# Attention's value products one loop step later, with operands shifted against their weights and gmlp pieces in another order

## The chip, the cores and the metric

The kernel runs on one core of one Trainium2 chip. The metric is the device time of one execution in microseconds. Engines: PE is TensorE (PEld its weight loads), DVE is VectorE, ACT is ScalarE, POOL is GpSimd, SP is SyncE, which here issues nearly all DMAs.

## What is computed

One layer of a decoder for 1,024 prompt positions and 64 sample positions (8 sequences of 8) that share weights, everything in float32. Of the reference, what bears on the change:

```python
h = rmsnorm(x, norm_mix)
q, k, v, gu, gv, ga, gb = split_in(h @ w_in)      # 16 query heads, 4 key/value heads of 64
o = attn_prompt(q, k, v, sinks)                   # window 128, blocks of 128 queries, 256 keys
s = spatial_gating(gelu(gu), layernorm(gelu(gv)), ws, bs)
merged = sigmoid(ga) * (o @ w_pa) + sigmoid(gb) * (s @ w_pb)
x = x + merged @ w_out
x = x + conv_ffn(rmsnorm(x, norm_ffn), ...)
```

In prompt attention a block of 128 queries sees its own block of keys up to the diagonal and the previous block's keys above it, so each query sees exactly 128 keys.

## The kernel before

A float32 product is made of three products in a rounded 32-bit form: every operand is split into a high part (a copy, on ScalarE) and a low part (a subtraction, on VectorE), and `wh*h + wh*l + wl*h` are summed in PSUM. Large products with 7 sub-products per tile pair come before and after; the change touches the stage between them, about 460 to 690 us into the span.

The positions are two groups: group 0 has the 64 sample positions and prompt blocks 0 to 3 (576 columns), group 1 prompt blocks 4 to 7 (512 columns). `attention(gr, pieces)` runs once for each group. It first does the sample attention (group 0 only), then a loop over 16 steps (4 key/value heads by 4 blocks), software-pipelined. In loop step i:

- `tr_p` transposes step i-2's normalized probabilities (four 128x128 transposes into the one bank `pt`), and splits them into `ph` (ScalarE) and `pl` (VectorE). From both GpSimd selects `c` with four affine selects: scores of one half of the previous and one half of the own block lie in the same 128 columns, and `c` holds, for the half where the two mix, the entries that belong to the other block.
- `sc_p` scores step i: eight matmuls with queries as weights and keys `kst` streaming into the one score buffer `sc`; a copy to `s` (ScalarE), a masked copy of the previous block's scores over it (VectorE), a maximum (VectorE), four exponentials (ScalarE), a reciprocal and a scaling (VectorE).
- `pv_p` multiplies step i-2's `ph` and `pl` by the values `vst` (four matmuls) and `c` by the difference of neighbouring blocks' values `dvst` (two matmuls), into the one bank `po`; then a copy (ScalarE), two additions and the split of the output (`oh`, `ol`).

In front of and behind `sc_p` stands `fill()`, which works off a list of pieces of other work, so that TensorE has something to do: as many as `slots["at"] * n // slots["of"]` says. For group 0 the pieces are the gmlp branch's products: `branch(c)` gives eight pieces for output tile c, four for each position group, each with nine matmuls; the first fetches the weight tile (`W.get`, which also casts the next one and loads further ones), the last of each group multiplies by the gate tile and stores the product to DRAM (`mbd`). The gate tile is loaded by `sg_load` into one of the four buffers of `stg`. For group 1 the pieces are the merge products of group 0's attention output.

Keys, queries and values of the next head are loaded from DRAM by `operands(kv + 1)` and `values(kv + 1)` within the steps of the current head; each has two buffers. The values were written to DRAM (`vd`, and their differences `dvd`) some 400 us earlier, one store for each block, in `v_out`.

The order of instructions on each engine's queue isn't the program's text alone: a scheduler reorders the text's instructions by what it takes to be ready, keeping the dependencies. `gap(pool, n)` is an unused tile of n bytes per partition, which moves the tiles behind it.

Of the kernel before, what the change touches and what calls it, by code (L numbers as in the profile page):

```python
# [6 lines left out]
F32 = mybir.dt.float32  # L7
# [8 lines left out]
P = 128  # L16
D = 1024
KD = 8
# [16 lines left out]
def layer(tc, a):  # L35
# [11 lines left out]
    with ExitStack() as top:  # L47
# [287 lines left out]
        vd = dr("vd", [P, NKV, 8, P])  # L335
        v3d = dr("v3d", [P, 256])
        dvd = dr("dvd", [P, NKV, 8, P])
# [14 lines left out]
        with ExitStack() as ph1:  # L352
# [175 lines left out]
            def v_out(g, i, ps):  # L528
# [7 lines left out]
                else:  # L536
# [3 lines left out]
                    for to, x in ((vd, v), (dvd, None)):  # L540
# [11 lines left out]
                        nc.sync.dma_start(to[:, :, name], t)  # L552
# [367 lines left out]
            def prepare(gr):  # L920
# [8 lines left out]
                def operands(kv):  # L929
                    def go():  # L930
                        if kv < NKV:
                            t = gr["kst"][kv] = kvp.tile([P, 2, nk], F32R, name="kst", bufs=2)
                            r = 64 * (kv % 2)
# [9 lines left out]
                def values(kv):  # L943

                    def go():
                        if kv < NKV:
# [3 lines left out]
                            nc.sync.dma_start(v.bitcast(F32), vd[:, kv, b0:b0 + nv])  # L950
                            for e in (0, 64):
                                for o in (0, 64):
                                    nc.sync.dma_start(d[o:o + 64, e // 64].bitcast(F32),
                                                      dvd[e:e + 64, kv, b0 + 1:b0 + 1 + nd])
# [77 lines left out]
            def sg_load(c):  # L1032
                for g in range(2) if c < KD else ():
                    n, off = groups[g]["n"], groups[g]["off"]
                    t = sgs[c, g] = stage(n)
                    nc.sync.dma_start(t, sgd[1][c][:, off:off + n])

            def branch(c):
# [3 lines left out]
                def part(g, e, k0):  # L1042
                    n, off, base = (groups[g][x] for x in ("n", "off", "base"))

                    def go():
# [4 lines left out]
                        if g == e == 0 and k0:  # L1050
                            sg_load(c + 1)
# [30 lines left out]
            def attention(gr, pieces):  # L1082
# [6 lines left out]
                slots = {"n": len(pieces), "done": 0, "at": 0, "of": 40 + (8 if has_s else 0)}  # L1089
# [99 lines left out]
                with tc.tile_pool(name=f"at{g}", bufs=1) as ap:  # L1189
                    steps = [(kv, i) for kv in range(NKV) for i in range(nblk)]  # L1190
                    st = {}

                    def sc_p(kv, i):
# [15 lines left out]
                        if i == 2:  # L1209
                            gr["values"](kv + 1)()  # L1210
                        s = ap.tile([P, 4, P + 1], F32, name="s", bufs=3)
# [18 lines left out]
                    def tr_p(kv, i):  # L1230
# [4 lines left out]
                        ph = ap.tile([P, 512], F32R, name="ph")  # L1235
                        pl = ap.tile([P, 512], F32R, name="pl")
                        split(ph, pl, pt)
                        parts = []
                        if gr["blk0"] + i:
                            c = ap.tile([P, 512], F32R, name="c")  # L1240
# [36 lines left out]
                    for i in range(len(steps) + 2):  # L1277
                        if i >= 2:
# [4 lines left out]
                        fill()  # L1283
                        if i >= 2:
                            pv_p(*steps[i - 2])
# [9 lines left out]
            sg_load(0)  # L1295
# [643 lines left out]
```

## Time and profile before

| | |
|---|---|
| time, median of 3 runs | 1530.84 us (1525.71 to 1532.65) |
| time of the profiled execution | 1529.31 us |
| its span | 1527.6 us |
| granted TensorE clock | 0.996 |
| PE busy | 1507.0 us (99%) |
| PEld busy | 1489.1 us (97%) |
| DVE busy | 1156.2 us (76%) |
| ACT busy | 823.2 us (54%) |
| POOL busy | 274.9 us (18%) |

The span is the time from the first to the last instruction of one profiled execution. A busy PE isn't PE at its peak, as matmuls are pipelined: idle weight loads and the mean duration of a matmul tell more. In a group's row, L and a number is the line of the kernel before, then engine, operation, output and inputs by the program's names, shapes, count, busy time, mean of one in ns, and the idle time of the engine just before them with what ended it. "A <- B: x, n, y" says that A waited for B for x us in all, n times, y at most. A row of one tile's instructions gives minimum, median and maximum of their durations.

### The profile page before, as it was taken

The numbers are of one execution on the slowest core, as the hardware profiler recorded it, in microseconds if no ns is written. First come the engines' busy times: TensorE is split into PE (matmuls) and PEld (weight loads), VectorE is DVE, ScalarE is ACT, GpSimd is POOL, SyncE is SP. The second block draws the span as 40 slices with busy tenths as digits, with TensorE's granted clock in tenths as the row PEclk, the third lists the DMA queues.
The fourth block names the chain that finished last, engine by engine and source line by source line (L and its number), as shares of the span: only waits on it lengthen the run. The fifth ranks groups of instructions, "written<-read, shape, count | busy, mean of one in ns | idle before, by whom it ended". The sixth has DMA issues, their size and how long they took to land.

```text
span 1527.6 us, 31403 instructions
## 1 busy us (share of the span) xinstructions
PE 1507.0 (99%) x12202; PEld 1489.1 (97%) x12202; DVE 1156.2 (76%) x1918; ACT 823.2 (54%) x1745; POOL 274.9 (18%) x429
## 2 busy tenths in 40 slices
PE   9999999999999999999999999999999999999998
PEld 9999999999998999989999999999999999999997
DVE  6886778756544886889658888898899888785685
ACT  6555764454543674774433555555555556453562
POOL 0000002200120232440122212232232222000002
PEclk9999999999999999999999999999999999999998
DMA  8553447747649857658988432332243226973453
GB/s 285 156 170 126 166 168 257 247 140 270 222 152 327 258 187 217 202 181 301 327 275 275 146 120 92 120 137 100 87 151 107 79 93 214 363 258 96 127 177 130
DMA packets 136357, 286.64 MB, mean 188 GB/s; under 512 B 15248, under 2 KB 43344, under 8 KB 136208
## 3 DMA queue, kind: packets, MB, share of 16 engines
q1 hardware_dynamic: 132176, 281.08, 55.2%
q10 hardware_dynamic: 4032, 3.55, 0.7%
q8 instruction: 96, 1.57, 0.4%
q14 instruction: 53, 0.43, 0.1%
HBM read 195.69 MB, written 90.85 MB: 188 GB/s over the span
## 4 chain that ended last, share of the span: by engine, by line
PE 68%; DVE 5%; ACT 4%; issue 3%; POOL 2%; DMA 2%; SPq 0%; POOLq 0%; ACTq 0%; DVEq 0%
PE st L294 40%; PE dn L1700 13%; PE mm L235 12%; ACT s L1224 2%; POOL c L1245 1%; POOL x L1765 1%; PE sc L1205 1%; PE mx L832 1%; DVE pl L41 1%; DVE nm L1221 1%; DVE s L1227 0%; ACT ot L1268 0%; DVE wl L41 0%; DVE of L1273 0%; DMA wraw<-wpb 0%
## 5 line engine op out<-in xcount | busy, mean ns | idle before, releaser
L294 PE MATMUL st<-th,wh 128*128 128x256 f32 (+1 forms) x2128 | 611.3, 287 | 4.2 <-ACT k L275 2.3
L294 PE MATMUL st<-tl,wh 128*128 128x256 f32 (+1 forms) x2128 | 609.4, 286 | 0.0
L294 PE MATMUL st<-th,wl 128*128 128x256 f32 (+1 forms) x2128 | 608.8, 286 | 0.0
L294 PEld LDWEIGHTS st<-th,wh 128*128 128x128 f32 x2128 | 400.7, 188 | 6.0 <-ACT k L275 3.4
L294 PEld LDWEIGHTS st<-th,wl 128*128 128x128 f32 x2128 | 401.0, 188 | 0.0
L294 PEld LDWEIGHTS st<-tl,wh 128*128 128x128 f32 x2128 | 400.5, 188 | 0.0
L40 ACT CAST wh<-wraw 128x512 fp32r<-128x512 f32 (+2 forms) x204 | 139.6, 694 | 107.0 <-PE st L294 35.4
L41 DVE TENSOR_TENSOR wl<-wraw,wh 128x512 fp32r<-128x512 f32 (+2 forms) x204 | 159.4, 794 | 37.7 <-ACT wh L40 35.5
L1700 PE MATMUL dn<-th,wh 128*128 128x288 f32 (+1 forms) x616 | 176.7, 287 | 0.0
L1700 PE MATMUL dn<-tl,wh 128*128 128x288 f32 (+1 forms) x616 | 176.2, 286 | 0.0
L1700 PE MATMUL dn<-th,wl 128*128 128x288 f32 (+1 forms) x616 | 175.1, 284 | 0.0
L40 ACT CAST wh<-ws 128x512 fp32r<-128x512 f32 x160 | 98.1, 622 | 96.8 <-PE st L294 62.0
L41 DVE TENSOR_TENSOR wl<-ws,wh 128x512 fp32r<-128x512 f32 x160 | 109.5, 697 | 48.5 <-ACT wh L40 46.8
L1700 PEld LDWEIGHTS dn<-th,wl 128*128 128x128 f32 x616 | 115.9, 188 | 0.0
L1700 PEld LDWEIGHTS dn<-tl,wh 128*128 128x128 f32 x616 | 115.7, 188 | 0.0
L1700 PEld LDWEIGHTS dn<-th,wh 128*128 128x128 f32 x616 | 115.6, 188 | 0.0
L282 POOL TENSOR_TENSOR z<-kn,k 128x256 f32<-128x256 f32 (+1 forms) x32 | 29.9, 938 | 320.0 <-ACT kn L277 304.4
L40 ACT CAST th<-traw 128x544 fp32r<-128x544 f32 (+1 forms) x85 | 53.8, 642 | 45.1 <-PE dn L1700 32.6
L41 DVE TENSOR_TENSOR tl<-traw,th 128x544 fp32r<-128x544 f32 (+1 forms) x85 | 61.6, 732 | 21.0 <-ACT th L40 20.6
L235 PE MATMUL mm<-s,wh 128*128 128x256 f32 (+1 forms) x384 | 75.4, 292 | 0.9 <-DMA s<-sd 0.9
L525 PE MATMUL st<-w2h,th 128*128 128x256 f32 x308 | 74.4, 283 | 0.4 <-ACT w2h L40 0.4
L235 PE MATMUL mm<-oh,wh 128*128 128x256 f32 (+1 forms) x256 | 74.0, 289 | 0.0
(292 smaller groups left out, 3178.2 us busy)
## 6 DMA issues: line engine op xcount, KB each, us to landing
wraw<-wt SPq DMA_DIRECT2D x133, 512.0 KB
traw<-td SPq DMA_DIRECT2D x77, 272.0 KB
td<-za SPq DMA_DIRECT2D x22, 544.0 KB
wraw<-wt SPq DMA_DIRECT2D x35, 256.0 KB
upd<-hl SPq DMA_DIRECT2D x14, 512.0 KB
td<-t SPq DMA_DIRECT2D x11, 544.0 KB
qd<-q SPq DMA_DIRECT2D x8, 576.0 KB
q<-qd SPq DMA_DIRECT2D x8, 576.0 KB
```

What stands on the lines that cost most here:

```text
L40: S.copy(hi, src)
L41: V.tensor_sub(lo, src, hi.bitcast(F32))
L235: PE.matmul(ps[:, lo:lo + c1 - c0], u[:, k, :], v[:, c0:c1], start=(k == 0 and i == 0), stop=(k == nk - 1 and i == 2))
L282: op(to, pick(x, to, lo, hi), pick(y, to, lo, hi))
L294: PE.matmul(ps, u[:, kk, :], v, start=first and kk + i == 0, stop=kk == 3 and i == 2, skip_group_check=True)
L525: PE.matmul(ps, u, v[:, k, :], start=k + i == 0, stop=k == KD - 1 and i == 2)
L832: PE.matmul(ps[:, P * i:P * i + P], vn[:, i], late["wst"][:, c, :], start=True, stop=True)
L1205: PE.matmul(ps[:, h, o0:256], q, kst[kv][:, e, k0:cur + P], start=e == 0, stop=e == 1)
L1221: V.tensor_reduce(nm, s, AX.X, ALU.max, negate=True)
L1224: S.activation(s[:, h], s[:, h], AF.Exp, bias=nm[:, h:h + 1], accum_out=dn[:, h:h + 1])
L1245: G.affine_select(cs[w:w + 64, :, e], src[r:r + 64, :, e].bitcast(F32), [[0, 4], [1 - 2 * e, 64]], ALU.is_ge, 0.0, base=-e, channel_multip ...
L1700: PE.matmul(place(m, e), u[:, m, :], v[:, lo:hi], start=new and i + k == 0 and (e == 0 or m % 2 == 0), stop=i == NU - 1 and k == 2, skip_g ...
```

## The change

1. In attention's loop `pv_p` works on step i-3 instead of i-2; the loop has one step more, `ph`, `pl` and `c` have two buffers, the next head's values are requested at its fourth block instead of the third, and the number of slots grows from 40 to 41.
2. `vd` and `dvd` are laid out by block: [8, P, NKV, P] instead of [P, NKV, 8, P].
3. A gap of 64 bytes behind the first key tile, gaps of 256 and 128 bytes ahead of attention's own tiles, and rows of `s` of 132 instead of 129 elements.
4. The gmlp pieces run for two output tiles c, c+1 at a time: group 0 of both, then group 1 of both. The gate tile of a tile and group is loaded at its own first piece, no longer in pairs within the tile before.

```diff
-        vd = dr("vd", [P, NKV, 8, P])
+        vd = dr("vd", [8, P, NKV, P])
...
-        dvd = dr("dvd", [P, NKV, 8, P])
+        dvd = dr("dvd", [8, P, NKV, P])
...
-                        nc.sync.dma_start(to[:, :, name], t)
+                        nc.sync.dma_start(to[name], t)
...
                             t = gr["kst"][kv] = kvp.tile([P, 2, nk], F32R, name="kst", bufs=2)
+                            if kv == 0:
+                                gap(kvp, 64)
...
-                            nc.sync.dma_start(v.bitcast(F32), vd[:, kv, b0:b0 + nv])
+                            nc.sync.dma_start(v.bitcast(F32), vd[b0:b0 + nv, :, kv].rearrange("b p d -> p b d"))
                             for e in (0, 64):
                                 for o in (0, 64):
                                     nc.sync.dma_start(d[o:o + 64, e // 64].bitcast(F32),
-                                                      dvd[e:e + 64, kv, b0 + 1:b0 + 1 + nd])
+                                                      dvd[b0 + 1:b0 + 1 + nd, e:e + 64, kv].rearrange(
+                                                          "b p d -> p b d"))
...
-            def sg_load(c):
-                for g in range(2) if c < KD else ():
-                    n, off = groups[g]["n"], groups[g]["off"]
-                    t = sgs[c, g] = stage(n)
-                    nc.sync.dma_start(t, sgd[1][c][:, off:off + n])
+            def sg_load(c, g):
+                n, off = groups[g]["n"], groups[g]["off"]
+                t = sgs[c, g] = stage(n)
+                nc.sync.dma_start(t, sgd[1][c][:, off:off + n])
...
-                        if g == e == 0 and k0:
-                            sg_load(c + 1)
+                        if e == k0 == 0:
+                            sg_load(c, g)
...
-                slots = {"n": len(pieces), "done": 0, "at": 0, "of": 40 + (8 if has_s else 0)}
+                slots = {"n": len(pieces), "done": 0, "at": 0, "of": 41 + (8 if has_s else 0)}
...
+                    gap(ap, (256, 128)[g])
...
-                        if i == 2:
+                        if i == 3:
                             gr["values"](kv + 1)()
-                        s = ap.tile([P, 4, P + 1], F32, name="s", bufs=3)
+                        s = ap.tile([P, 4, 132], F32, name="s", bufs=3)[:, :, 0:P + 1]
...
-                        ph = ap.tile([P, 512], F32R, name="ph")
-                        pl = ap.tile([P, 512], F32R, name="pl")
+                        ph = ap.tile([P, 512], F32R, name="ph", bufs=2)
+                        pl = ap.tile([P, 512], F32R, name="pl", bufs=2)
...
-                            c = ap.tile([P, 512], F32R, name="c")
+                            c = ap.tile([P, 512], F32R, name="c", bufs=2)
...
-                    for i in range(len(steps) + 2):
-                        if i >= 2:
+                    for i in range(len(steps) + 3):
+                        if 2 <= i < len(steps) + 2:
                             tr_p(*steps[i - 2])
                         fill()
                         if i < len(steps):
                             sc_p(*steps[i])
-                        fill()
-                        if i >= 2:
-                            pv_p(*steps[i - 2])
+                        if i < len(steps) + 2:
+                            fill()
+                        if i >= 3:
+                            pv_p(*steps[i - 3])
...
-            sg_load(0)
-            attention(groups[0], [x for c in range(KD) for x in branch(c)])
+            parts = [branch(c) for c in range(KD)]
+            attention(groups[0], [x for c in range(0, KD, 2) for g in (0, 4) for d in (0, 1) for x in parts[c + d][g:g + 4]])
```

## The prediction

> **What bounds the kernel now.** I read the page's busy line first, then a table of stretches around attention, then who the weight loads waited for, then the groups of matmuls by shape, then the chain of work.
>
> ```profile
> span 1527.6 us, 31403 instructions
> PE 1507.0 (99%) x12202; PEld 1489.1 (97%) x12202; DVE 1156.2 (76%) x1918; ACT 823.2 (54%) x1745; POOL 274.9 (18%) x429
> ```
>
> TensorE has work in flight nearly all the time, so no part of the change can win more than TensorE's own stalls and slow matmuls in the stage that it touches. That stage is attention, one stretch for each position group:
>
> ```profile
> core 0: us, PE busy (x) PEld busy (x) DVE busy (x) ACT busy (x) POOL busy (x), PEclk, DMA share, GB/s
> 500.00:582.00 82.00, 80.17 (x615) 75.67 (x615) 70.21 (x131) 59.72 (x192) 25.67 (x61) 1.00 0.63 209
> 600.00:687.00 87.00, 84.43 (x622) 78.80 (x621) 74.98 (x140) 64.08 (x198) 34.86 (x77) 1.00 0.66 204
> ...
> 630.00:660.00 30.00, 29.10 (x215) 27.28 (x213) 27.30 (x53) 23.65 (x75) 13.08 (x30) 1.00 0.76 249
> 688.00:784.00 96.00, 95.95 (x769) 95.90 (x769) 64.92 (x87) 39.84 (x56) 12.44 (x9) 1.00 0.88 311
> ```
>
> Columns after the stretch: its length, then busy time of each engine. The weight loads (PEld) are the better gauge: in the pure product stage 688 to 784 they are busy 95.90 of 96, in attention 75.67 of 82 and 78.80 of 87. So attention leaks about 6 and 8 us in weight loads that stand still. The clock is 1.00 throughout. VectorE is second: 86% of either stretch, and 27.30 of 30 (91%) at its fullest. Whom the loads waited for, from 460 to 690:
>
> ```profile
> PEld po L1265 <- POOL c L1245: 7.6, 25, 1.1
> PEld po L1262 <- DVE pl L41: 1.5, 4, 0.5
> PEld mm L235 <- DMA s<-sd: 1.4, 2, 0.8
> PEld po L1262 <- issue: 1.1, 4, 0.4
> PEld po L1262 <- ACT ph L40: 0.8, 2, 0.5
> ```
>
> The largest by far is the value product waiting for `c`, the part of the probabilities that GpSimd selects for the previous block's difference.
>
> **Term A: value products one step later.** In one loop step the kernel transposes the probabilities of block i-2 (`tr_p`), fills, scores block i (`sc_p`), fills, then multiplies i-2's probabilities with the values (`pv_p`). Between `tr_p` and `pv_p` lies this chain:
>
> ```profile
> L1245 POOL TENSOR_SCALAR_AFFINE_SELECT c<-ph x56: 408/413/877, 508.9 to 684.1; 64x256 fp32r<-64x256 f32 x56
> L1245 POOL TENSOR_SCALAR_AFFINE_SELECT c<-pl x56: 409/412/1279, 510.4 to 685.2; 64x256 fp32r<-64x256 f32 x56
> L40 ACT CAST ph<-pt x32: 567/587/592, 505.4 to 683.0; 128x512 fp32r<-128x512 f32 x32
> L41 DVE TENSOR_TENSOR pl<-pt,ph x32: 675/692/694, 506.3 to 683.8; 128x512 fp32r<-128x512 f32 x32
> ```
>
> With medians: 0.587 (ACT) + 0.692 (VectorE) + 2 x 0.412 (the two selects that need `pl`) = 2.1 us even if every engine is free. VectorE is 86% busy, so it often isn't. After the change a whole step more lies between: there are 32 steps in 82 + 87 us, so about 5.3 us. The chain then has some 8 us and is no longer late. What its lateness costs, from the groups by shape (mean ns, then the idle time before them):
>
> ```profile
> L1265 PE MATMUL po<-c,dvst 128*128 128x256 f32 x56 | 18.4, 353 | 2.7 <-POOL c L1245 1.7
> L1262 PE MATMUL po<-ph,vst 128*128 128x256 f32 x56 | 16.2, 295 | 0.6 <-ACT ph L40 0.2
> L1262 PE MATMUL po<-pl,vst 128*128 128x256 f32 x56 | 15.2, 294 | 0.7 <-DVE pl L41 0.7
> L235 PE MATMUL mm<-mh,wh 128*128 128x256 f32 x192 | 53.5, 279 | 0.0
> L1205 PE MATMUL sc<-kst,q 128*128 128x256 f32 x224 | 32.8, 286 | 0.2 <-ACT s L1213 0.2
> ...
> L1262 PEld LDWEIGHTS po<-ph,vst 128*128 128x128 f32 x56 | 10.6, 189 | 2.1 <-issue 1.1 <-ACT ph L40 0.8 <-ACT s L1213 0.2
> L1262 PEld LDWEIGHTS po<-pl,vst 128*128 128x128 f32 x56 | 10.5, 188 | 1.8 <-DVE pl L41 1.5
> L1265 PEld LDWEIGHTS po<-c,dvst 128*128 128x128 f32 x56 | 10.0, 187 | 8.4 <-POOL c L1245 7.6
> ```
>
> Idle in front of these weight loads: 8.4 + 2.1 + 1.8 = 12.3 us. A load that waited also can't run ahead of the matmul before it, so the matmul behind it shows longer: 56 x (353 - 279) + 56 x (295 - 279) + 56 x (294 - 279) ns = 4.1 + 0.9 + 0.8 = 5.8 us. Upper end 18.1 us.
>
> The lower end comes from VectorE, which does the same work in less time. If it can't go beyond the 91% of its fullest stretch, the two stretches shrink to 70.21 / 0.91 = 77.2 and 74.98 / 0.91 = 82.4, a gain of 4.8 + 4.6 = 9.4 us. Part of VectorE's idleness is itself due to the late products:
>
> ```profile
> ACT ot L1268 <- PE po L1265: 26.2, 19, 2.8
> ```
>
> ```profile
> DVE of L1273 <- ACT ot L1268: 8.3, 12, 1.9
> DVE dn L1226 <- ACT s L1224: 7.6, 11, 1.7
> ```
>
> ScalarE stood 26.2 us in front of the output copy of a product that wasn't there, with the next step's exponentials queued behind it, and VectorE waited for both. So VectorE should get a little past 91%, though not far: I take **11 us**, nearer to the VectorE end, which is 92.5 to 93% of either stretch. What is late next is VectorE's `pl`, which frees the single transpose bank, and its masked copy, which frees the single score bank. One more loop step (19 instead of 18) adds a fill and no work; `ph`, `pl`, `c` double, so the early split waits for no product.
>
> **Term B: 192 modulo 256.** `kst` buffers are 2 x 512 x 4 or 2 x 640 x 4 bytes, queries 2 x 576 x 4 or 2 x 512 x 4, block steps 512 bytes, all multiples of 256. So keys (streamed) and queries (weights) now start a multiple of 256 bytes apart. The gap of 64 bytes behind the first keys changes that; gaps and the wider `s` move the probabilities against the values. If this is why a score matmul shows 286 ns and an equal-sized output product 279, it is worth 224 x 7 ns = 1.6 us at the upper end; the same 7 ns on the 168 value products, 1.2 us more. The lower end is nothing, or as much lost, -2.8 us. I take 0.5, since most of it would hide behind VectorE. The Trainium skill, "TensorE: Matmul & The Clock Gate", Part 2, on loading the stationary operand, gives TensorE two independent read ports, one for the streamed operand and one for the weights, so that neither takes bandwidth from the other; by that rule this part changes nothing, and the sum would be 0.5 us smaller. No row here separates addresses from shapes, so the trace leaves this open.
>
> **Term C: gmlp pieces by group for two tiles.** The chain shows the second group's operands arriving late, and a loader that blocks the queue:
>
> ```profile
> 467.64 5.28 DMA s<-sd
> ...
> 540.20 2.00 DMA mbd<-stg
> 542.22 0.32 SPq L1036
> 542.63 4.44 DMA wraw<-wt
> ```
>
> The new order runs two tiles of group 0 before it touches group 1's operands: four more pieces of 9 matmuls, some 5 us of cover, so the 1.4 us of weight loads waiting for `s` should mostly go. Second, the gate loads now need the buffer of four groups ago instead of the one just stored:
>
> ```profile
> SPq L1036 <- DMA mbd<-stg: 4.2, 6, 1.5
> SPq L950 <- PE po L1265: 7.8, 3, 5.0
> ```
>
> So 4.2 us of queue blocking goes, with weights queued behind it in the lines at 542. Casts for the second weight tile come four pieces after the first instead of eight, and both tiles stay until the pair is done: three of the ring's four slots. Ends: -1 and 2 us; I take 1.
>
> **Term D: values by block.** Stores before attention become one run of 2,048 bytes per partition instead of four of 512; loads become four or five runs of 512 instead of one.
>
> ```profile
> L552 SPq DMA_DIRECT2D vd<-ws x8: 513/516/617, 45.9 to 87.5; - x8
> L950 SPq DMA_DIRECT2D vst<-vd x8: 319/345/631, 475.5 to 646.5; - x8
> L953 SPq DMA_DIRECT2D dvst<-dvd x32: 444/541/1445, 477.3 to 649.1; - x32
> ```
>
> A four-run issue took 516 ns, a one-run issue 345. The value loads should go to about 516: 8 x 0.17 = 1.4 us of SyncE's queue. The 32 difference loads, by the same step, cost 5.4 us of that queue at most; the 15 stores give 2.6 us back. Behind them in the queue stand weights and keys, but these loads are issued four steps (20 us) before their use, as before: the request moves one step later together with the products, and its wait for the products that free the buffer (7.8 us above) keeps its form. On the path I put -0.5 us, between -3 and 1.
>
> **Sum.** 11 + 0.5 + 1 - 0.5 = 12 us. The profiled execution took 1529.31 us beside its span of 1527.6; less 12 is 1517.3. The median of the runs shown (1530.84) lies 1.5 above that execution, so I predict 1518.8 us. The runs before spread over 1525.71 to 1532.65, so half a per cent, 7.65 us, is about what a measurement of this kernel can tell from no change.
>
> **Rivals.**
>
> 1. The wait moves to VectorE. The score and transpose banks are single, so TensorE stops there as soon as VectorE lags. For it: 91% in the fullest stretch. Against it: the waits for VectorE at scores and transposes are below 1 us each now. If only 4 us of A survive and B hides, 4 + 1 - 0.5 = 4.5, so 1526.3: no change that can be told.
> 2. VectorE keeps up entirely, the whole upper end is won: 18.1 + 1.5 + 1 = 20.6, so 1510.2.
> 3. Slower: gate tiles late. They were loaded in pairs a whole tile ahead, now at the first piece of their own group, and the product with them stands in VectorE's strict order ahead of softmax work. Groups follow each other by
>
> ```profile
> 499.53 0.75 DVE L1055 TENSOR_TENSOR stg<-stg,mm 128x576 f32<-128x576 f32 x1 [0.44 <-PE mm L235]
> 587.01 0.69 DVE L1055 TENSOR_TENSOR stg<-stg,mm 128x512 f32<-128x512 f32 x1 [1.01 <-PE mm L235]
> ```
>
>    (587.01 - 499.53) / 11 = 8.0 us, so the load has about 6 us. A small store landed in 2.00 us, a 512 KB weight load in 4.44. It decides from a landing of over 6 us: with 8 us, each of 16 groups holds VectorE 2 us, 32 us in all, against the 12 won: 1530.8 + 20 = 1551. Were half of them late, 1535.
> 4. The change doesn't do what it says: the order of TensorE's queue is planned with assumed costs, and the products are pulled forward again to where `c` is late; then B, C and D remain, 1 us: 1529.8.
>
> **How the numbers follow.** Forecast (1513 to 1523) 0.52; rival 2 0.12; rival 1 0.20; rival 4 0.09; rival 3 0.07. Faster by over half a per cent: forecast and rival 2, 0.64. Same: rivals 1 and 4, 0.29. Slower: 0.07. The range runs from rival 2's 1510 to 1528, which leaves out rival 3, most of rival 4 and the tail of rival 2, under 2 in 10.
>
> **What would show it.** A: the wait of value products for GpSimd's `c` is gone and the c product's mean falls from 353 to about 285 ns; both attention stretches shrink 5 to 6 us, and VectorE's share there rises to about 93%. B: the score matmul's mean falls from 286 toward 279. C: no weight load waits for `s`, no gate load for a store. D: value-load issues near 516 ns and no product waiting for a value DMA. It would be wrong if new waits of scores or transposes on VectorE add up to more than 5 us, or if VectorE waits for a gate tile's DMA.

## The result, and the profile after

| | before | after |
|---|---|---|
| median, first comparison | 1529.7 us (21 runs) | 1524.99 us (21 runs, 1519.64 to 1529.17) |
| ratio, 95% interval | | 0.9966 (0.9955 to 0.9976) |
| median, in a later comparison | 1529.93 us (20 runs) | 1521.57 us (9 runs) |
| ratio, 95% interval | | 0.995 (0.9931 to 0.9969) |
| profiled execution, its span | 1529.31, 1527.6 us | 1525.18, 1523.3 us |

The change makes the kernel faster, by 4.7 us in the first comparison and 8.4 in the later one. The intervals of the two overlap from 0.9955 to 0.9969, some 5 to 7 us. The forecast was 12. Three profiles of the changed kernel end at 1523.3, 1519.3 and 1528.4 us, so single executions say little about 2 or 3 us; the times below are medians against the kernel before on the same chip, and the traces are read for what waits for what.

The page's busy line after, then the stretches of attention (same columns as before):

```profile
span 1523.3 us, 31416 instructions
PE 1500.1 (98%) x12202; PEld 1486.9 (98%) x12202; DVE 1155.1 (76%) x1918; ACT 822.8 (54%) x1745; POOL 273.1 (18%) x429
```

```profile
500.00:582.00 82.00, 78.42 (x627) 75.60 (x626) 70.37 (x132) 60.91 (x193) 29.06 (x64) 1.00 0.66 221
600.00:687.00 87.00, 84.03 (x656) 80.90 (x655) 76.45 (x144) 65.11 (x200) 31.36 (x77) 1.00 0.69 214
```

In the same two stretches TensorE now does 627 + 656 matmuls instead of 615 + 622, 3.7% more. VectorE's share is 86% and 88%; it was 86% and 86%. The forecast had counted on 92.5 to 93%.

Whom TensorE waited for, from 460 to 690 (line numbers of the changed kernel: 1237 is the transposes, 1265 and 1268 the value products):

```profile
PE pt L1237 <- DVE s L1230: 3.1, 5, 1.3
PEld pt L1237 <- ACT ot L1271: 3.0, 3, 1.4
PEld pt L1237 <- issue: 2.4, 6, 1.0
PEld mm L235 <- DMA s<-sd: 2.2, 1, 2.2
...
PEld po L1265 <- issue: 1.6, 3, 0.7
PEld pt L1237 <- DVE pl L41: 1.1, 2, 0.7
PE po L1265 <- DVE of L1276: 1.0, 3, 0.5
...
PE pt L1237 <- DVE pl L41: 0.7, 2, 0.5
...
PEld sc L1208 <- DVE s L1218: 0.2, 1, 0.2
```

The wait for GpSimd's `c` that led the list before (7.6 us) is gone, and the transposes have taken its place. The groups by shape, from 490 to 690 (mean ns, then idle before):

```profile
L1268 PE MATMUL po<-c,dvst 128*128 128x256 f32 x56 | 11.2, 281 | 0.0
L1265 PE MATMUL po<-ph,vst 128*128 128x256 f32 x56 | 15.4, 296 | 2.1 <-DVE of L1276 1.0 <-ACT s L1216 0.6 <-ACT s L1227 0.4
L1265 PE MATMUL po<-pl,vst 128*128 128x256 f32 x56 | 14.6, 282 | 0.0
L1208 PE MATMUL sc<-kst,q 128*128 128x256 f32 x224 | 32.0, 283 | 0.0
L1237 PEld LDWEIGHTS pt<-c_ident,s 128*128 128x128 f32 x128 | 13.9, 141 | 7.4 <-ACT ot L1271 3.0 <-issue 2.4 <-DVE pl L41 1.1
L1265 PEld LDWEIGHTS po<-ph,vst 128*128 128x128 f32 x56 | 10.5, 188 | 3.3 <-issue 1.6 <-ACT s L1216 0.8 <-ACT s L1227 0.6
L1265 PEld LDWEIGHTS po<-pl,vst 128*128 128x128 f32 x56 | 10.6, 189 | 0.0
L1268 PEld LDWEIGHTS po<-c,dvst 128*128 128x128 f32 x56 | 8.6, 189 | 0.0
```

The loads of the value products stood 12.3 us before and 3.3 now, and the c product takes 281 ns instead of 353. The same row of the kernel before for the transposes:

```profile
L1234 PE MATMUL pt<-c_ident,s 128*128 128x128 f32 x128 | 20.2, 273 | 0.6 <-DVE s L1227 0.5
L1234 PEld LDWEIGHTS pt<-c_ident,s 128*128 128x128 f32 x128 | 14.8, 140 | 1.8 <-ACT s L1213 0.7 <-issue 0.6
```

So 9.0 us of standing loads went at the value products and 5.6 came back at the transposes. How much of this is time is worked out with the first experiment.

### The profile page after: what moved, and what is told of

It reads as the page before. It is cut to its first block, busy times and chain, and to the rows that moved or that the text cites. A ratio compares the mean times of both kernels' runs of the same rounds, so it can differ in the third digit from the quotient of the medians.

```text
span 1523.3 us, 31416 instructions
## 1 busy us (share of the span) xinstructions
PE 1500.1 (98%) x12202; PEld 1486.9 (98%) x12202; DVE 1155.1 (76%) x1918; ACT 822.8 (54%) x1745; POOL 273.1 (18%) x429
## 4 chain that ended last, share of the span: by engine, by line
PE 65%; DVE 7%; DMA 4%; ACT 3%; issue 3%; POOL 1%; SPq 0%; POOLq 0%; DVEq 0%; ACTq 0%
PE st L294 40%; PE mm L235 13%; PE dn L1704 10%; DMA wraw<-wt 2%; DVE wl L41 1%; ACT s L1227 1%; POOL x L1769 1%; PE sc L1208 1%; PE mx L832 1%; DVE s L1230 1%; DMA s<-sd 1%; DVE nm L1224 1%; ACT wh L40 1%; DMA wraw<-wpb 1%; DVE s L1218 1%
## 5 line engine op out<-in xcount | busy, mean ns | idle before, releaser
L235 PE MATMUL mm<-ol,wh 128*128 128x256 f32 (+1 forms) x256 | 73.7, 289 | 0.3 <-DVE ol L41 0.3
```

The costliest lines, as they stand in the source:

```text
L235: PE.matmul(ps[:, lo:lo + c1 - c0], u[:, k, :], v[:, c0:c1], start=(k == 0 and i == 0), stop=(k == nk - 1 and i == 2))
```

## Experiments

Two figures go with each run. "Stage" is the time from the first score of the samples to the first product of the merged tiles, worked out from the start times of these two instructions in its trace; the matmuls in it are the same in number and shape in every kernel. In the three profiles of the changed kernel it is 258.6, 259.1 and 261.2 us, so 2 or 3 us in this column can belong to one execution. "Idle" is the time that weight loads stood, from 490 to 690, in front of value products / transposes / scores, added from the rows by shape.

| kernel | median (before on that chip) | ratio, 95% interval | stage | idle |
|---|---|---|---|---|
| before | | | 263.2 | 12.4 / 1.8 / 1.1 |
| after | 1524.99 (1529.7) | 0.9966 (0.9955 to 0.9976) | 258.6 | 3.3 / 7.4 / 0.9 |
| A alone | 1524.47 (1529.54) | 0.9965 (0.9951 to 0.998) | 258.6 | 4.1 / 7.9 / 1.5 |
| B alone | 1528.28 (1529.54) | 0.9997 (0.9981 to 1.0012) | 262.7 | 12.5 / 1.8 / 1.1 |
| C alone | 1533.49 (1529.54) | 1.0024 (1.0007 to 1.0041) | 264.6 | 14.5 / 1.7 / 1.1 |
| D alone | 1530.56 (1529.54) | 1.0 (0.9983 to 1.0017) | 263.1 | 12.5 / 1.6 / 2.1 |
| A, `ol` on GpSimd | 1522.98 (1530.29) | 0.9953 (0.9936 to 0.9969) | 257.9 | 3.6 / 5.2 / 0.3 |
| before, `ol` on GpSimd | 1533.61 (1530.29) | 1.0026 (1.0009 to 1.0042) | 267.7 | 18.0 / 0.9 / 0.6 |
| A, transposes later too | 1522.15 (1530.29) | 0.9959 (0.9943 to 0.9974) | 254.9 | 3.2 / 4.0 / 2.7 |
| A, B with mended gaps | 1525.44 (1530.29) | 0.9971 (0.9957 to 0.9984) | 260.9 | 4.2 / 8.2 / 1.0 |
| A, more for VectorE | 1527.23 (1529.14) | 0.9986 (0.9973 to 0.9998) | 262.0 | 5.1 / 7.9 / 1.4 |
| A, more for ScalarE | 1524.49 (1529.14) | 0.9964 (0.9949 to 0.998) | 259.1 | 3.7 / 6.7 / 1.8 |
| A, transposes later, `ol` on GpSimd | 1524.7 (1529.14) | 0.9967 (0.9952 to 0.9982) | 261.7 | 4.4 / 6.0 / 1.7 |
| before, short weight splits | 1523.85 (1529.31) | 0.9962 (0.9948 to 0.9976) | 256.9 | 8.4 / 1.8 / 0.1 |
| A, short weight splits | 1519.38 (1529.31) | 0.9934 (0.9916 to 0.9951) | 253.8 | 3.1 / 3.9 / 0.4 |
| after, `ol` on GpSimd | 1520.45 (1529.31) | 0.9939 (0.9923 to 0.9956) | 255.7 | 1.8 / 7.5 / 0.6 |
| after, transposes later | 1524.4 (1529.31) | 0.9966 (0.9949 to 0.9982) | 258.8 | 5.8 / 3.3 / 2.9 |
| after, `wl` on GpSimd | 1530.58 (1529.93) | 1.0003 (0.9987 to 1.0018) | 265.6 | 8.2 / 7.5 / 1.4 |

**1. The four parts, each alone.** Theory T1: the wait moved. T2: A is worth its 11 us and another part takes them back. T3: the gain is from the other parts.

A, value products one step later:

```diff
-                    for i in range(len(steps) + 2):
-                        if i >= 2:
+                    for i in range(len(steps) + 3):
+                        if 2 <= i < len(steps) + 2:
                             tr_p(*steps[i - 2])
...
-                        if i >= 2:
-                            pv_p(*steps[i - 2])
+                        if i >= 3:
+                            pv_p(*steps[i - 3])
```

> The kernel before with the value products one loop step later and nothing else. Theory 1, the wait moved: the products' wait for GpSimd's selected probabilities goes (8.4 us of weight-load idle to under 1), but the transposes then wait for the probabilities that VectorE scales, 3 us or more, as in the changed kernel; net gain of the two attention stretches 3 to 5 us. Theory 2, this part is worth the forecast's 11 us and another part takes some 6 us back: attention 9 to 12 us shorter here. Theory 3, the gain comes from the other parts: attention within 1 us of before.

B, the gaps and the 132 columns:

```diff
+                            if kv == 0:
+                                gap(kvp, 64)
...
+                    gap(ap, (256, 128)[g])
...
-                        s = ap.tile([P, 4, P + 1], F32, name="s", bufs=3)
+                        s = ap.tile([P, 4, 132], F32, name="s", bufs=3)[:, :, 0:P + 1]
```

> The kernel before with the three gaps and the wider rows of the scores and nothing else. Theory 1: the mean start to start of a 256-column score matmul falls by about 3 ns, as in the changed kernel, so under 1 us in all, and the value products stay as they are. Theory 2 with this part as the one that takes back: attention longer by several us. Theory 3 with this part as the gain: 3 to 5 us shorter.

C, the order of the gmlp pieces and the gate loads:

```diff
-            attention(groups[0], [x for c in range(KD) for x in branch(c)])
+            parts = [branch(c) for c in range(KD)]
+            attention(groups[0], [x for c in range(0, KD, 2) for g in (0, 4) for d in (0, 1) for x in parts[c + d][g:g + 4]])
```

> The kernel before with the gmlp pieces by group for two tiles and the gate tiles loaded at their own first piece, and nothing else. Theory 1: within 1.5 us of before; the wait for the gmlp operands at the start of the stage stays about as it is (0.5 to 2 us), since it ends when that DMA lands, whatever comes after. Theory 2 with this part as the one that takes back: attention longer by 2 to 6 us, with VectorE waiting for gate tiles. Theory 3: 3 to 5 us shorter.

D, values by block:

```diff
-        vd = dr("vd", [P, NKV, 8, P])
+        vd = dr("vd", [8, P, NKV, P])
```

> The kernel before with the values stored and loaded by block and nothing else. Theory 1: the start of attention moves by up to 2 us (in the changed kernel's profile it began 2.1 us earlier), but the gmlp operands land no earlier, so less than 1 us of it is left when the first scores start. Theory 2 with this part as the one that takes back: value products wait for their values' DMA, attention 2 to 6 us longer. Theory 3: 2 to 5 us shorter over all.

A alone has the whole gain of the first comparison (5.1 us), B and D are none that can be told, C alone is slower by 4 us, where T1 had it within 1.5 us of before. For A, T1 holds; T2 and T3 fall. The rows of A alone, from 490 to 690:

```profile
L1234 PE MATMUL pt<-c_ident,s 128*128 128x128 f32 x128 | 19.9, 278 | 4.6 <-DVE s L1227 2.4 <-DVE pl L41 1.9
L1262 PE MATMUL po<-ph,vst 128*128 128x256 f32 x56 | 15.6, 299 | 3.0 <-DVE of L1273 1.5 <-ACT s L1213 1.1 <-ACT s L1224 0.4
L1262 PE MATMUL po<-pl,vst 128*128 128x256 f32 x56 | 14.8, 286 | 0.0
L1234 PEld LDWEIGHTS pt<-c_ident,s 128*128 128x128 f32 x128 | 14.0, 141 | 7.9 <-issue 2.9 <-ACT ot L1268 1.7 <-DVE pl L41 1.4
L1265 PE MATMUL po<-c,dvst 128*128 128x256 f32 x56 | 11.3, 284 | 0.0
...
L1262 PEld LDWEIGHTS po<-ph,vst 128*128 128x128 f32 x56 | 10.8, 193 | 4.1 <-ACT ph L40 1.4 <-ACT s L1213 1.3 <-issue 0.7
```

Loads of the value products stand 12.3 - 4.1 = 8.2 us less than before, those of the transposes 7.9 - 1.8 = 6.1 us more. That isn't time one for one: before, the loads of the value products stood 12.3 us, but TensorE's matmuls only 2.7 + 0.6 + 0.7 = 4.0. The time can be added up from start to start: each matmul is given the time from the start of the matmul before it to its own start, and over the stage these times add up to the stage. From the start times in the traces, in us:

| matmuls | before | A alone | after |
|---|---|---|---|
| value products | 33.7 | 26.5 | 25.3 |
| transposes (8 of the samples' among them) | 19.7 | 23.2 | 22.6 |
| scores | 31.9 | 32.2 | 31.0 |
| gmlp and merge products | 169.6 | 168.4 | 171.9 |
| the rest of the samples' | 8.3 | 8.3 | 7.9 |
| stage | 263.2 | 258.6 | 258.6 |

In the three profiles of the changed kernel the value products take 25.2 to 25.8 us, the transposes 22.2 to 23.4, the gmlp and merge products 170.6 to 173.6; so differences of up to 3 us in those last products tell nothing. A alone won 7.2 us at the value products and gave back 3.5 at the transposes and 0.3 at the scores; with 1.2 us at the gmlp and merge products, within their spread, that is 4.6, and the medians differ by 5.1. So the mechanism was right and the price of what is late next was missing.

Why C alone is slower wasn't separated further. Its profiled execution is the fastest of its twelve (1528.79), so the trace shows only a part: a stage 1.5 us longer, with 598 matmuls from 500 to 582 instead of 615, and

```profile
PEld po L1264 <- POOL c L1244: 8.7, 28, 1.1
```

so the value products wait longer for `c` than before (7.6 us, 25 times). VectorE waits for no gate tile's DMA in that stage. With A the wait for `c` is gone, and with it probably most of C's cost; that was not run by itself.

**2. What holds the transposes: VectorE's work, or delay?** Theory 1a: VectorE's throughput. Theory 1b: delay along the chain, through in-order queues and single banks.

```diff
-                        split(oh[kv][:, :, c0:c0 + P], ol[kv][:, :, c0:c0 + P], of)
+                        S.copy(oh[kv][:, :, c0:c0 + P], of)
+                        G.tensor_sub(ol[kv][:, :, c0:c0 + P], of, oh[kv][:, :, c0:c0 + P].bitcast(F32))
```

> Value products one step later (A), and the low part of attention's output, ol = of - oh (32 subtractions of some 490 ns on VectorE in the two attention stretches), is computed on GpSimd instead. A alone ran at 1524.5 us, 5.1 under the kernel before; 12 us of waits of value products and transposes above the usual step remain in it. Theory 1a, what is left is VectorE's throughput (145.9 of 169 us busy in the stretches): 15 us less work for it gives another 3 to 6 us, 1518.5 to 1521.5, and VectorE's waits at transposes and products fall. Theory 1b, what is left is delay along the chain through the queues of ScalarE and VectorE: within 1.5 us of A alone, 1523 to 1526, since GpSimd does the same subtraction no sooner. Should GpSimd share a port with VectorE and slow it, slower than A alone.

The same two lines in the kernel before:

> The control: the kernel before, value products where they were, with the same subtraction on GpSimd. If VectorE's load bounds attention whichever way the products stand (1a), it gains 3 to 6 us by itself: 1524 to 1527. If the wait for c bounds it, GpSimd has 32 more instructions in the same queue as the selects that make c: no gain, or 1 to 3 us slower, 1529.5 to 1532.5.

On A 15 us less for VectorE bring 1.2 permille against A alone, which the intervals don't separate from nothing; the time, 1522.98, lies between the two ranges. On the kernel before it costs 0.26%, a little more than was expected: the subtractions (946 ns each on GpSimd) stand in front of the selects, and loads of value products stand 18.0 us. VectorE's own instructions keep their lengths beside them: with the subtraction on GpSimd `pl` took 690 ns and the maximum 679, the same as in A alone, the scaling of the probabilities 738 against 712. The Trainium skill, "Perfetto Trace Analysis", Optimizing Scalar/DVE Operations, warns that GpSimd and VectorE share a read port of SBUF, so that moving work from one to the other might not help; here the traces show at most the 26 ns of the scaling for that (on the changed kernel the same edit brought it from 732 to 719), and what differs between the two kernels is what stands behind the moved instruction in GpSimd's queue.

Transposes a step later:

```diff
-                        if 2 <= i < len(steps) + 2:
-                            tr_p(*steps[i - 2])
+                        if 3 <= i < len(steps) + 3:
+                            tr_p(*steps[i - 3])
...
-                        if i >= 3:
-                            pv_p(*steps[i - 3])
+                        if i >= 4:
+                            pv_p(*steps[i - 4])
```

> A, and the transposes of the probabilities a further step later too (scores of block i, transposes of i-3, value products of i-4; four score buffers in place of three, values requested one step later). No engine has more or less to do. Theory 1b (delay): the transposes no longer wait for VectorE's normalisation of the probabilities (2.4 us in A) and ScalarE's queue gets slack, another 2 to 5 us: 1519.5 to 1522.5. Theory 1a (throughput of VectorE): the wait only moves to the single banks; within 1.5 us of A alone, 1523 to 1526.

The wait for the normalized probabilities is gone, and the banks come next:

```profile
L1234 PE MATMUL pt<-c_ident,s 128*128 128x128 f32 x128 | 19.4, 274 | 2.5 <-DVE pl L41 2.5
L1262 PE MATMUL po<-ph,vst 128*128 128x256 f32 x56 | 15.0, 290 | 2.5 <-DVE of L1273 2.5
L1234 PEld LDWEIGHTS pt<-c_ident,s 128*128 128x128 f32 x128 | 14.6, 140 | 4.0 <-issue 1.5 <-PE po L1265 1.3 <-DVE pl L41 0.6
L1205 PEld LDWEIGHTS sc<-kst,q 128*128 128x128 f32 x256 | 32.6, 190 | 2.7 <-DVE s L1215 2.0
```

`pl` reads the transpose bank, `of` the product bank, the masked copy (L1215) the score bank: each of the three stops its TensorE step now. Start to start the transposes take 19.3 us instead of A's 23.2, the scores 33.7 instead of 32.2. In time it is 2.3 us under A alone by the medians, 0.9 by the ratios, within both intervals; on the changed kernel (below) the same edit brought nothing.

Work added to A, first for VectorE:

```diff
                         split(oh[kv][:, :, c0:c0 + P], ol[kv][:, :, c0:c0 + P], of)
+                        more = ap.tile([P, 2, P], F32, name="more")
+                        V.tensor_sub(more, of, oh[kv][:, :, c0:c0 + P].bitcast(F32))
```

> A, and on VectorE one more subtraction of 128x256 in each of the 32 steps, whose result nobody reads: 15 us of extra work, put behind the low part of the attention output. Theory 1a (A stands at VectorE's throughput): VectorE goes from 86 to about 92% of the stretches and most of the 15 us shows, 7 to 15 us slower than A alone: 1531.5 to 1539.5. Theory 1b (delay in a ring of single banks and in-order queues): some of it shows, since the later instructions of the queue shift by half a microsecond in each step, but not more than what the same time on ScalarE costs: 3 to 8 us.

Then for ScalarE:

```diff
                         split(oh[kv][:, :, c0:c0 + P], ol[kv][:, :, c0:c0 + P], of)
+                        more = ap.tile([P, 2, P], F32, name="more")
+                        S.copy(more, of)
```

> A, and on ScalarE one more copy of 128x256 in each step, whose result nobody reads: 32 x 0.4 = 13 us of extra work on an engine that is 74% busy in the stretches. Theory 1a: ScalarE isn't the bound, within 2 us of A alone, 1523 to 1526.5. Theory 1b: the queue of ScalarE lies in the ring (copy of the scores, four exponentials, cast of the transposed, copy of the product) as VectorE's does, so it costs as much as on VectorE, 3 to 8 us: 1527.5 to 1532.5.

The 15 us for VectorE cost 2.8 us against A alone by the medians (1527.23 to 1524.47; the two intervals overlap a little), the 13 us for ScalarE nothing. The stretches of the first (A alone, too, has a clock of 0.98 in the second):

```profile
500.00:582.00 82.00, 76.32 (x612) 73.69 (x610) 74.17 (x143) 59.62 (x192) 29.13 (x60) 1.00 0.64 211
600.00:687.00 87.00, 83.75 (x643) 81.47 (x642) 77.74 (x155) 64.23 (x198) 31.62 (x77) 0.98 0.70 217
```

VectorE can be 90% busy here, so at 86 to 88% it isn't full: four fifths of what is added goes into its idle time. 1a falls as the bound. What 1b said of ScalarE (3 to 8 us) fell as well.

A with both earlier edits, the transposes later and `ol` on GpSimd:

> A with the transposes a step later and the low part of the output on GpSimd, which alone gave 1522.2 and 1523.0 against 1524.5 for A. If VectorE's throughput and the delay are two limits of which either hides the gain of the other, together they give more than their sum, 5 us or more below A: 1515 to 1519.5. If the gains only add: 1520 to 1521.5. If GpSimd, now with the selects and the subtraction, becomes the late engine: no better than either, 1522 to 1524.

Both reliefs together are no better than A alone, and above all three ranges; the gains, if they are any, don't add. Its profile has the stage at 261.7, with 33.3 us instead of 28.9 in the sample part that neither edit touches, so it says little of the reason.

**3. The addresses.** From the addresses of the tiles: before, keys and queries lie 0 modulo 256 apart, probabilities and values 32, the gmlp operands and weights 192. After, keys and queries lie 192 apart, but probabilities and values 128 in group 0 and 0 in group 1, and the wider tiles and gaps also moved the gmlp operands of group 1 to 0. From the trace, matmuls that follow one another start 119.3 ns apart for scores before and 116.0 after; gmlp products of group 1 went from 115.8 to 118.9. So an offset of 192 came out about 3 ns shorter than 0 with 256 columns: 224 x 3.3 ns = 0.7 us won and 288 x 3.1 ns = 0.9 us lost. The 20 profiles agree: scores start 119.1 to 119.6 ns apart in the 12 with offset 0 and 115.8 to 116.7 in the 8 with 192. Within the changed kernel's own profile the gmlp products of group 0, still at 192, start 115 ns apart beside 118.9 in group 1. For matmuls of 256 columns only 0 and 192 were compared so plainly; that 256 bytes is the period isn't shown. The mended gaps:

```diff
-                    gap(ap, (256, 128)[g])
+                    gap(ap, (384, 64)[g])
...
             m1 = mo[1].enter_context(tc.tile_pool(name="mlp1", bufs=1, reuse_waits="tile"))
+            gap(m1, 192)
```

> A, and the address part with its gaps chosen so that it does what it says: keys 192 modulo 256 off the queries, probabilities and c 192 off the values in both groups, and the second group's gmlp operands left at 192 (the change had the probabilities at 128 and 0 and the gmlp operands at 0). If the offset is worth the 3 ns that the score matmul gained in the changed kernel: 256 scores and 176 value products get 3 ns faster, 1.3 us, of which the value products' half depends on how 32 stood before; 1523 to 1524 against A alone at 1524.5, with the score matmul near 116 ns start to start and the second group's gmlp matmuls near 116 as before. If the offset does nothing: equal to A alone, 1524.5.

All offsets are 192 there, the scores start 115.8 to 116.2 ns apart and take

```profile
L1209 PE MATMUL sc<-kst,q 128*128 128x256 f32 x224 | 32.0, 283 | 0.3 <-DMA q<-qd 0.3
```

yet the time is no better than A alone. The scores do get shorter, 31.2 us start to start instead of A's 32.2; 1 us is less than these comparisons can tell, and where it went isn't shown.

**4. The long instructions of the weight splits.** In A's trace some of the longer waits (up to 1.3 us) lie next to casts of 1.05 us (ScalarE) and their subtractions of 1.25 us (VectorE). Theory L: these make what is left. Theory R: the ring of softmax steps does.

```diff
-                        split(h[:, 0:k], l[:, 0:k], t[:, 0:k, :])
+                        m = 1 if self.light else k
+                        split(h[:, 0:m], l[:, 0:m], t[:, 0:m, :])
```

On A:

> A, and the 17 or so gmlp weight tiles that attention's stages split into a high and a low part are split in their first 128 of 768 or 1024 columns only; the gmlp products then use that first block for all (so their output is another; the matmuls, loads and stores are the same in number and shape). That takes some 15 us of ScalarE (casts of 1.05 us) and 17 us of VectorE (subtractions of 1.25 us) out of the two stretches, all of it in long instructions. Theory L (the long casts bunch the queues: the waits of 1.3 us that are left in A lie next to them): most of those waits go, 3.5 to 6.5 us under A alone, 1518 to 1521. Theory R (what is left is the ring of softmax steps through single banks, whatever else the engines do): within 1.5 us of A alone, 1523 to 1526; the +15 us on VectorE that cost 3 us and the +13 us on ScalarE that cost nothing speak for R.

On the kernel before:

> The kernel before with the same reduced splits. If the lateness of c is due to the long casts too (c waits for pl, and pl for VectorE's queue), it gains as much as A does, 3 to 6 us: 1523.5 to 1526.5. If c is late by the plain length of its chain (0.587 + 0.692 + 2 x 0.412 us): within 1.5 us of the kernel before, 1528 to 1531.

Shortening them is worth 5.1 us on A and 5.5 on the kernel before, though it takes less work away than expected: 14 tiles in the traces, 9 us of ScalarE and 12 of VectorE. So L is right on what those instructions cost. But A itself is worth 4.5 us with short splits (1523.85 to 1519.38) and 5.1 with long ones, so they don't explain why A fell short of its forecast. Start to start both sides of A's balance shrink: with short splits it wins 5.1 us at the value products (30.2 to 25.1) and gives back 1.6 at the transposes and scores, with long ones 7.2 and 3.8. In the kernel before with short splits the wait for `c` is still first:

```profile
L1269 PEld LDWEIGHTS po<-c,dvst 128*128 128x128 f32 x56 | 10.1, 187 | 6.6 <-POOL c L1249 5.7
```

By the time, 1523.85, the first of the two expectations for this run holds, that the long casts make `c` late. By the rows they make only a part of it: the loads in front of the c product stand 6.6 us instead of 8.4, and the gain is spread over the whole ring (start to start 3.5 us at the value products, 1.8 at the transposes, 0.9 at the scores).

**5. On the changed kernel.**

The edits of `ol` and of the transposes, each put on the changed kernel:

> The changed kernel with the low part of attention's output on GpSimd, a candidate that should beat both kernels. If the gain that this gave on A alone (1523.0 against 1524.5) is real: 1521 to 1523.5. If it was within the noise: 1524 to 1525.5.

> The changed kernel with the transposes a step later too, the other candidate. If the gain on A alone (1522.2 against 1524.5) is real: 1520.5 to 1523. If it was within the noise: 1524 to 1525.5.

And the low parts of the weights on GpSimd, within the steps only:

```diff
-                        split(h[:, 0:k], l[:, 0:k], t[:, 0:k, :])
+                        if self.light:
+                            S.copy(h[:, 0:k], t[:, 0:k, :])
+                            G.tensor_sub(l[:, 0:k], t[:, 0:k, :], h[:, 0:k].bitcast(F32))
```

> The changed kernel, with the low part of the gmlp weight tiles that attention's steps split computed on GpSimd instead of VectorE: 17 subtractions of some 1.2 us leave VectorE's queue, the casts of 1.05 us stay on ScalarE. By the 964 ns that GpSimd took for 128x256, estimated 3 to 4 us each there, in front of the selects for c, which have a step of 5 us to spare. If the long instructions in VectorE's queue are what the reduced splits won (5 us): 1520 to 1522.5. If it was the casts on ScalarE, or if GpSimd now holds c and the weights up: 1524 to 1529.

> The changed kernel itself on the same chip, for a direct comparison: 0.9955 to 0.9976 of the kernel before, 1523 to 1526, its last stage in either rhythm.

With the transposes later the time is in the range for no gain, with `ol` on GpSimd half a microsecond below the range for a real one; the changed kernel by itself came out at 1521.57 and 0.995, faster than expected. The version with `ol` on GpSimd is the fastest full kernel by its ratio, 0.9939, 8.9 us under the kernel before; against the changed kernel (0.9966 and 0.995) the intervals touch, so that it beats that too isn't shown. With `wl` on GpSimd the kernel is 9.0 us slower than the changed kernel on the same chip, slower than either expectation, and the wait for `c` is back:

```profile
L201 POOL TENSOR_TENSOR wl<-wraw,wh 128x1024 fp32r<-128x1024 f32 x8 | 19.2, 2405 | 17.8 <-ACT wh L200 10.9 <-DVE s L1223 4.7 <-issue 1.6
L1273 PE MATMUL po<-c,dvst 128*128 128x256 f32 x56 | 12.8, 301 | 3.5 <-POOL c L1253 3.3
L1273 PEld LDWEIGHTS po<-c,dvst 128*128 128x128 f32 x56 | 9.1, 192 | 4.8 <-POOL c L1253 4.8
```

GpSimd takes 2.4 us for such a subtraction and stood 17.8 us in front of these eight, most of it until the cast was done. With selects queued behind them, the step that A had won for `c` no longer suffices; that the queue is the reason is inferred from these rows. Whether the 5 us of the short splits came from VectorE's or from ScalarE's share of them stays open.

The changed kernel once more, for its profile:

> The changed kernel once more, for its profile. In the last weight stage (the dn products) the profile of the changed kernel and that of the address part alone ran a slower rhythm, 233.87 and 233.86 us from the first product to the last, against 230.80 in the kernel before and in most others, though the instructions there are the same. If that belongs to the program: 233.9 again. If it is chance of an execution: 230.8 or 233.9.

From its first product to its last, the last weight stage took 230.80 us this time, as in the kernel before, against 233.87 in the first profile of the same kernel. So that difference of 3 us between the profiles isn't the change's.

## Why the prediction was wrong, step by step

**Term A, 11 us forecast, 5.1 measured, is the step that failed.** Its mechanism came as told: the wait for `c` is gone, the c product's mean fell from 353 to 281 (about 285 forecast). What failed is the sentence on what is late next. It named the banks, but put no price on them; the price was taken from VectorE's share of the stretch, as if VectorE's work were the only thing between TensorE and the gain. The runs put 3.8 us there: of the 7.2 us that A alone won at the value products start to start, 3.5 came back at the transposes, for the normalized probabilities, the bank and the queues, and 0.3 at the scores. VectorE's share stayed at 86 to 88% and can go to 90%. The "lower end" of 9.4 us was therefore no bound: a share reached in one stretch doesn't say that a chain of dependent steps lets the engine reach it in another. Nor does the share named for 11 us belong to it: 145.2 us of VectorE in 169 - 11 us is 91.9%, not 92.5 to 93.

The upper end was mis-sized as well. It adds longer matmuls (5.8 us) to standing loads (12.3 us), and both show the same delay. The 176 value products took 33.7 us start to start; 18.1 less would be 89 ns for each, while products of 256 columns start 113.6 ns apart in the faster rhythm of the last weight stage. Taking the products with `c`, `ph` and `pl` each from the profile where they take least (6.5, 8.3 and 7.9 us) gives 22.7, so some 11 us could be won at the value products. The forecast of 11 us is thus all of that, with nothing late behind it. A alone won 7.2; most of the rest stands at the product with `ph` (11.2 us against 8.3), which waits for `of`, the reader of the product bank, and for ScalarE.

**Rival 1** (the wait moves, 4 us of A are left, 1526.3) is nearest, with 5.1 left. Its name was half right: the wait moved, but to the transposes and the chain before them; VectorE's load made little of it. The waits of transposes and scores for VectorE add up to 5.1 us (3.1 + 0.7 + 1.1 + 0.2) and were 1.2 before (0.5 + 0.7), so 3.9 of them are new, under the 5 us that was set as the mark.

**Rival 2** assumed nothing back; **rival 3** didn't come: a gate tile's DMA held VectorE once, for 3.2 us in the window:

```profile
DVE stg L1077 <- DMA stg<-sg0d: 3.2, 1, 3.2
```

(that is a merge's gate, not the gmlp's). **Rival 4** didn't come either: A's edit shows in the order and in the time.

**Term B, 0.5 us forecast.** The score matmul went from 286 to 283, not 279, and the gaps did only a part of what the words say. By itself it is worth nothing that can be told, mended or not. By the rule of the Trainium skill that the prediction set beside it ("TensorE: Matmul & The Clock Gate", Part 2, two independent read ports), as it was applied there, nothing should change; the time agrees, but the start-to-start times of 119.3 and 116.0 ns don't: with the offset at 192 a score matmul takes 3% less.

**Term C, 1 us forecast.** The queue was freed for the most part:

```profile
SPq L1038 <- DMA mbd<-stg: 1.6, 2, 1.0
SPq L952 <- PE po L1268: 14.9, 2, 9.9
```

(4.2 us before; the wait of the value loads for their buffer grew from 7.8 to 14.9 and no matmul waited for it.) The wait of loads for `s` didn't go: 2.2 us once instead of 1.4 in two. In the first profile the samples' stage began 2.1 us earlier than before, and the operands landed no sooner; over all profiles that stage began between 460.0 and 464.9 us, with B alone at 461.6, so its start says nothing of C. Alone C costs 0.24%.

**Term D, -0.5 us forecast, nothing measured.** The value loads issue in 380 ns, not 516; the difference loads in 608:

```profile
L952 SPq DMA_DIRECT2D vst<-vd x8: 370/380/447, 474.4 to 646.2; - x8
L955 SPq DMA_DIRECT2D dvst<-dvd x32: 573/608/1657, 475.7 to 649.4; - x32
```

A row of stores with four runs was the wrong neighbour for a load with four.

## What to carry to other kernels

When a wait is taken away from a step in a pipelined ring, price the next wait before summing: take the row of every other step of the ring, and ask how much earlier the engine will stand there. Here half of what was won at one step (3.8 of 7.2 us) came back at the next. Count a delay once, too: a load that stands and a matmul that looks longer behind it can be the same time, and the times from start to start tell. A second engine's share of the stretch is no bound from either side; a run that adds work to it that nobody needs tells in one go whether it is full.

## What was not expected of the hardware

The last weight stage runs in one of two rhythms, in the same program at full granted clock. Matmuls counted from 1290 to 1450 us, in the kernel before, the first profile after and the second:

```profile
1290.00:1450.00 160.00, 160.00 (x1306) 160.00 (x1306) 115.92 (x202) 72.05 (x130) 0.00 (x0) 1.00 0.64 208
```

```profile
1290.00:1450.00 160.00, 160.00 (x1285) 160.00 (x1284) 113.52 (x202) 71.76 (x129) 0.00 (x0) 1.00 0.63 209
```

```profile
1290.00:1450.00 160.00, 160.00 (x1306) 160.00 (x1306) 114.30 (x204) 73.66 (x132) 0.00 (x0) 1.00 0.64 213
```

21 matmuls of 1306 fewer, at a clock of 1.00 throughout; it makes 3.1 us over the stage. In the faster rhythm the products of 256 columns start 113.6 ns apart, in the slower 117.3; those of 288 columns 132.2 in both. Which rhythm comes isn't settled by the program; what does settle it stays open. The merge products of 256 columns show much the same two, 114.6 ns apart in the first profile of the changed kernel and 117.4 in the second, so 3 ns between two executions don't by themselves belong to a change. The offset of the streamed operand against its weights is another matter: 192 bytes instead of 0 went with 3 ns of 116 to 119 in the scores and the gmlp products of 256 columns, in every profile.
